# An encoder layer's FFN: loads of the next weight pair ahead of the stores, residual loaded into the sums, four early weight sums on VectorE

## The chip, the core and the metric

The kernel runs on one NeuronCore of a Trainium2 chip. The core has five engines that run at the same time, each with its own in-order list of instructions: TensorE (PE in the profile; PEld is its weight load), VectorE (DVE), ScalarE (ACT), GpSimd (POOL) and SyncE (SP), which here issues nearly all DMA transfers. The metric is the device time of one execution in microseconds (us); lower is better.

## The reference

Two requests of 1024 tokens (`x_prompt`, `x_sample`) go through one post-norm encoder layer with the same weights. The attention part takes about a third of the kernel's code and isn't touched here. The part that the change touches is the last one:

```
D_MODEL, D_FF, SEQ = 1024, 4096, 1024
x = layer_norm(ALPHA * x + merged @ w_out, ln1_g, ln1_b)
hid = square(relu(x @ w_ff1 + b_ff1))                          # FFN layer 1: 1024 -> 4096
x = layer_norm(ALPHA * x + hid @ w_ff2 + b_ff2, ln2_g, ln2_b)  # FFN layer 2: 4096 -> 1024
```

All of it is float32. The term `ALPHA * x + b_ff2` that is added to the second product is called the residual below.

## The kernel before

The two requests (batches, `b` = 0 and 1) are worked through one after the other by the same code. Every float32 product is made of three products of a high and a low part (`mm3`, lines 107 to 109: hi x hi, lo x hi, hi x lo). `split` (line 745) makes the parts: ScalarE copies the high part (line 746), VectorE subtracts it for the low part (line 103, the helper `sub`).

A matrix product is done by Strassen's scheme in Winograd's form: seven products of half-size blocks instead of eight, with sums of blocks before and after.

**FFN layer 1** runs over `NP` = 16 pairs `p` of 128-column blocks of `w_ff1`. A pair has two loads of 512 KB, `top` (tile `w1t`, two buffers) and `bot` (tile `w1b`, one buffer). `job_a` makes products 1 and 2 from `top`. `job_b` makes the sums of blocks (tile `ss`, line 905 on), their splits (`oh`, `ol`; for the block `a22` the tiles `o`), five more products and the sums behind them, and writes seven blocks (`c11`, `ht`) to HBM with `put` (line 878). `job_a` of the first four pairs (`EARLY`) is done ahead. The tile `w1b` is last read by the split of `a22`, so the next `w1b` load has to wait for that split on VectorE.

In the pairs 4 to 11, behind each job, one eighth of the residual is made (lines 949 to 962): `rg` (scale and shift, broadcast over the partitions, two loads of 256 KB) and `rr` (512 KB of the normalised rows, tensor `resd`) are loaded, GpSimd multiplies and adds in four operations, and the result is stored back into `resd`.

**FFN layer 2** runs over four chunks `c` of 1024 rows of `w_ff2`, in each over the seven products m = 1, 2, 6, 5, 3, 7, 4 with two halves `u`, and four token tiles `t`. `operands` loads the weights (tile `rw`) and the hidden blocks (tile `hr`), forms sums of weight blocks (called T sums; `ts` and rewritten `rw`), and splits. For the first chunk the sums of `u` = 0 are on VectorE and those of `u` = 1 on GpSimd (line 1009); later chunks have both on GpSimd. `product` adds each product to `acc` in SBUF with VectorE (line 1052). In the first chunk the first addition to each quarter of `acc` reads the residual instead of `acc`: it is loaded for that, in sixteen loads of 256 KB (tile `r`, three buffers, line 1051).

**What sets the order.** The kernel is written with a scheduler that simulates the program and writes each engine's list in the order that comes out; the order of the source gives the priorities. SyncE's list is then worked off strictly in order: a DMA whose wait isn't over holds up every DMA behind it.

Of the kernel before, what the change touches and what calls it, by code (L numbers as in the profile page):

```python
# [9 lines left out]
F32 = mybir.dt.float32  # L10
# [71 lines left out]
def encoder_kernel(ctx, tc, xs, w_in, b_gate, w_a, w_b, w_out, rpb, ln1_g, ln1_b, w1, b1, w2, b2,  # L82
# [184 lines left out]
    for b, x in enumerate(xs):  # L267
# [627 lines left out]
        zp.release()  # L895
        pup = pool("pu", 1, side="right")
        htp = pool("ht", 8, side="right")

        def job_b(p, top, px, c11):
            bot = bop.tile([P, KT, P], F32, name="w1b", tag="w1b")  # L900
            nc.sync.dma_start(bot, w1[:, (2 * p + 1) * P:(2 * p + 2) * P].rearrange("(k p) c -> p k c", p=P))
            ss = sp_.tile([P, 4, 4, P], F32, name="ss", tag="ss")
            s2, s1, s3, s4 = (ss[:, i] for i in range(4))
            a11, a12, a21, a22 = top[:, :4], top[:, 4:], bot[:, :4], bot[:, 4:]
            nc.vector.tensor_tensor(s1, a21, a22, op=ALU.add)
            sub(nc.vector, s2, s1, a11)
            sub(nc.vector, s3, a11, a21)
            sub(nc.vector, s4, a12, s2)
            o65 = w1_ops(ss[:, 0:2].rearrange("p i k c -> p (i k) c"), nc.vector)
            o73 = w1_ops(ss[:, 2:4].rearrange("p i k c -> p (i k) c"), nc.vector)  # L910
            o4 = [opq.tile([P, 4, P], F32R, name=f"o4{s}", tag=f"o4{s}") for s in range(2)]
            split(*o4, a22, nc.vector)
            relu2(c11, c11, 2 * p)
            put(p, 1, c11)
            u2, u3, p5 = (pup.tile([P, 512], F32, name=n, tag=n) for n in ("u2", "u3", "p5"))
            prod(px, [t[:, :4] for t in o65], xb[6], False)
            nc.scalar.copy(u2, px)
            py = psy.tile([P, 512], F32, name="py", tag="py")
# [17 lines left out]
            sub(nc.vector, h2, h1, c11)  # L936
            put(p, 6, h2)
            sub(nc.vector, h3, c11, c12)
            put(p, 7, h3)
            sub(nc.vector, h4, c21, h2)  # L940
            put(p, 3, h4)

        for p in range(EARLY):
            job_b(p, w1_top(p), *early[p])
        for p in range(EARLY, NP):
            top = w1_top(p)
            job_b(p, top, *job_a(p, top))

            i = p - EARLY
            if i < 8:  # L950
                ns = slice(512 * (i // 4), 512 * (i // 4 + 1))
                its = slice(2 * (i % 4), 2 * (i % 4) + 2)
                gt = xp.tile([P, 2, 512], F32, name="rg", tag="x")
                for j in range(2):
                    v = agd[j, ns]
                    nc.sync.dma_start(gt[:, j], bass.AP(tensor=v.tensor, offset=v.offset, ap=[[0, P], [1, 512]]))
                rt = xp.tile([P, 2, 512], F32, name="rr", tag="x")
                nc.sync.dma_start(rt, resd[b][its, :, ns].rearrange("t p c -> p t c"))
                for j in range(2):
                    nc.gpsimd.tensor_tensor(rt[:, j], rt[:, j], gt[:, 0], op=ALU.mult)  # L960
                    nc.gpsimd.tensor_tensor(rt[:, j], rt[:, j], gt[:, 1], op=ALU.add)
                nc.sync.dma_start(resd[b][its, :, ns].rearrange("t p c -> p t c"), rt)
        psz.release()
        psy.release()
        psx.release()
        for q in (htp, pup, opq, opp, awp, c11p, sp_, bop, xbp):
            q.release()


# [4 lines left out]
        ac0p = pool("acc0")  # L974
        acc = [pl.tile([P, 4, 2, 512], F32, name=f"acc{i}") for i, pl in enumerate((ac0p, accp))]

        padp = pool("pad")
        padp.tile([P, 512], F32, name="pad")
        w2b = pool("w2b", 2)
        w2a = pool("w2a", 2, side="right")  # L980
        hrp = pool("hr", 4, side="right")
        w2r = pool("w2r", 2, side="right")
        rsp = pool("res", 3, side="right")
        jkp = pool("junk", side="right")
        psx = pool("ps_x", 4, space=PSUM)
        psr = pool("ps_r", 2, space=PSUM)
# [8 lines left out]
        for c in range(nch):  # L995
# [7 lines left out]
            def operands(n, m, u):  # L1003
                w = rw[u]
                for j, d in {1: ((0, 0),), 2: ((1, 0),), 6: ((0, 1), (1, 1))}.get(m, ()):
                    w[j, d] = (w2r if d else w2b if j else w2a).tile([P, 2, 512], F32, name=f"rw{j}{d}", tag=f"rw{j}{d}")
                    nc.sync.dma_start(w[j, d], w2v[u, j, :, :, 512 * d:512 * (d + 1)])
                b11, b12, b21, b22 = (w.get(i) for i in ((0, 0), (0, 1), (1, 0), (1, 1)))
                eng = nc.gpsimd if c or u else nc.vector
                if m == 6:  # L1010
                    for i in (5, 6):
                        w[i] = w2r.tile([P, 2, 512], F32, name=f"ts{i}", tag=f"ts{i}")
                    sub(eng, w[5], b12, b11)
                    sub(eng, w[6], b22, w[5])
# [12 lines left out]
                split(o[:, 0], o[:, 1], hr, nc.vector)  # L1027
                split(o[:, 2], o[:, 3], src, nc.vector)

            def product(m, t):  # L1030

                if m == 1:
                    px[t] = psx.tile([P, 512], F32, name="px", tag="px")
                if m in (1, 6, 7, 4):
                    ps = px[t]
                else:
                    pl, tag = ((pst, "pt"), (psr, "pr"))[t % 2]
                    ps = pl.tile([P, 512], F32, name=tag, tag=tag)
                cs = slice(t * P, (t + 1) * P)
                for u in range(2):  # L1040
                    o = ops[m, u]
                    for q in range(2):
                        mm3(ps, o[:, 0, q, cs], o[:, 1, q, cs], o[:, 2, q], o[:, 3, q], m not in (6, 7, 4) and u + q == 0,
                            u + q == 2, skip=True)
                for s_ in {1: (0,), 2: (0,), 6: (1,), 5: (1, 3), 3: (1,), 7: (3,), 4: (2,)}[m]:
                    a = acc[s_ // 2][:, t, s_ % 2]
                    r = a
                    if c == 0 and (m, s_) in ((1, 0), (6, 1), (5, 3), (4, 2)):
                        r = rsp.tile([P, 512], F32, name="r", tag="r")
                        ns = slice(512 * (s_ % 2), 512 * (s_ % 2 + 1))  # L1050
                        nc.sync.dma_start(r, resd[b][t + 4 * (s_ // 2), :, ns])
                    nc.vector.tensor_tensor(a, r, ps, op=ALU.add)
                if last and (m == 3 or m == 4 and b + 1 == len(xs)):
                    finish(m == 4, t)

            for n, m in enumerate((1, 2, 6, 5, 3, 7, 4)):
                for u in range(2):
                    operands(n, m, u)
                if not last or n < 5:
                    for t in range(4):  # L1060
                        product(m, t)
# [4 lines left out]
        psr.release()  # L1066
        psx.release()
        pst.release()
        for q in (jkp, rsp, w2r, hrp, w2a, w2b, padp, ac0p):
            q.release()  # L1070
        if b + 1 == len(xs):
            lnp.release()
# [41 lines left out]
```

## Time and profile before

| | us |
|---|---|
| median of 3 runs | 3175.51 |
| range of the runs | 3169.77 to 3178.15 |
| the profiled execution, its own time | 3184.45 |
| span of the profiled execution | 3182.6 |
| TensorE busy in it | 2951.2 (93% of the span) |
| VectorE / ScalarE / GpSimd busy | 1881.0 / 1449.7 / 979.1 |

Times in the trace count from the start of the span. FFN layer 1 of the first batch stands at about 950 to 1283 us and layer 2 at 1283 to 1500 us and on; of the second batch at about 2510 to 2840 us and 2840 to 3165 us. A row of the timeline gives the start, the duration, the engine, the line, the operation, the tiles, and in brackets how long the engine was idle before it and what ended that. SPq is SyncE's queue of DMA issues: its duration is that of the issue, not of the transfer. The view of stretches gives for each stretch the busy time of each engine with the number of its instructions, TensorE's granted clock as a share of full speed, the mean busy share of the DMA engines, and GB/s.

### The profile page before, as it was taken

To read this page: it belongs to the slowest core of one execution; us is meant where nothing else is said; L and a number is where in the kernel's file an instruction comes from. 1 tells how busy PE (TensorE), PEld (TensorE's weight loads), DVE (VectorE), ACT (ScalarE), POOL (GpSimd) and SP (SyncE) were. 2 spreads that over 40 slices of the span, in tenths; PEclk is the share of its full clock that TensorE was granted. 3 is DMA by queue.
4 is the path that set the end of the run, shared out by engine and by line. 5 is a ranking of instruction groups with operands and counts; after the bars stand their busy time and mean duration, and the time that the engine had idled before them with its cause. 6 is when DMAs were issued, how large, how long until landed. Compare 5 with 4: busy or idle time off the path is not lost. (4 is left out here: it accounts for less than half of the span.)

```text
span 3182.6 us, 39432 instructions
## 1 busy us (share of the span) xinstructions
PE 2951.2 (93%) x13964; PEld 2441.7 (77%) x13964; DVE 1881.0 (59%) x3439; ACT 1449.7 (46%) x2640; POOL 979.1 (31%) x716
## 2 busy tenths in 40 slices
PE   7879898999997899899989998989999979998997
PEld 7757786888786788688878786878877767886886
DVE  1036566673465666687861565567444756558887
ACT  3136564554363455333441564646542735553333
POOL 3464563223203200133341655432130131004322
PEclk9989898999998999899999999989999989999998
DMA  8742224345546644654354123244454575466442
GB/s 182 255 130 81 74 71 119 119 131 189 174 143 189 201 159 159 237 177 155 96 195 141 56 79 90 66 135 121 158 157 151 169 226 191 146 210 208 148 139 86
DMA packets 404414, 470.22 MB, mean 148 GB/s; under 512 B 44841, under 2 KB 282225, under 8 KB 403961
## 3 DMA queue, kind: packets, MB, share of 16 engines
q1 hardware_dynamic: 377720, 429.43, 43.1%
q10 hardware_dynamic: 26496, 38.28, 3.6%
q8 instruction: 110, 1.80, 0.2%
q14 instruction: 88, 0.71, 0.1%
HBM read 326.77 MB, written 141.79 MB: 147 GB/s over the span
## 5 line engine op out<-in xcount | busy, mean ns | idle before, releaser
L107 PE MATMUL pmm<-bh,whi 128*128 128x512 f32 x1152 | 465.4, 404 | 29.5 <-ACT r L451 23.6
L108 PE MATMUL pmm<-bh,wlo 128*128 128x512 f32 x1152 | 463.2, 402 | 0.0
L109 PE MATMUL pmm<-bl,whi 128*128 128x512 f32 x1152 | 462.7, 402 | 0.0
L103 POOL TENSOR_TENSOR wlo<-wraw,whi 128x512 fp32r<-128x512 f32 (+1 forms) x176 | 231.8, 1331 | 533.0 <-ACT whi L195 493.1
L107 PEld LDWEIGHTS pmm<-bh,whi 128*128 128x128 f32 x1152 | 221.1, 192 | 72.8 <-ACT r L451 24.9
L109 PEld LDWEIGHTS pmm<-bl,whi 128*128 128x128 f32 x1152 | 220.9, 192 | 42.7
L108 PEld LDWEIGHTS pmm<-bh,wlo 128*128 128x128 f32 x1152 | 221.0, 192 | 40.3
L103 POOL TENSOR_TENSOR ts<-rw,rw 128x1024 f32<-128x1024 f32 x14 | 41.4, 2957 | 655.7 <-DMA rw<-in_w_ff_dram 497.4
L746 ACT CAST bh<-hr 128x1024 fp32r<-128x1024 f32 x56 | 58.7, 1048 | 366.0 <-PE px L109 216.9
L391 ACT ACTIVATE smk<-smk,nm 128x256 f32<-128x256 f32 (+4 forms) x320 | 162.0, 508 | 129.1 <-DVE nm L390 126.1
L103 DVE TENSOR_TENSOR ptl<-pt,pth 128x512 fp32r<-128x512 f32 (+3 forms) x224 | 125.3, 569 | 67.4 <-ACT pth L667 36.7
L107 PE MATMUL psv<-wv,bh 128*128 128x384 f32 (+1 forms) x384 | 139.7, 365 | 19.8 <-DVE vt L103 18.2
L103 DVE TENSOR_TENSOR vt<-psv,vt 128x384 fp32r<-128x384 f32 (+1 forms) x48 | 28.8, 602 | 214.4 <-ACT vt L342 214.4
L108 PE MATMUL psv<-wv,bl 128*128 128x384 f32 (+1 forms) x384 | 139.9, 364 | 0.3 <-DVE bl L103 0.3
L109 PE MATMUL psv<-wv,bh 128*128 128x384 f32 (+1 forms) x384 | 138.5, 363 | 1.6 <-POOL wv L103 1.5
L107 PE MATMUL px<-bh,oh 128*128 128x512 f32 x256 | 106.4, 416 | 32.4 <-ACT oh L746 25.3
L103 POOL TENSOR_TENSOR qs<-r,qs 64x512 fp32r<-64x512 f32 x80 | 116.8, 1460 | 63.2 <-ACT qs L414 58.9
L108 PE MATMUL px<-bh,ol 128*128 128x512 f32 x256 | 105.6, 413 | 20.1 <-DVE ol L103 20.1
L746 ACT CAST oh<-ss 128x1024 fp32r<-128x1024 f32 x64 | 66.9, 1053 | 123.9 <-DVE ss L103 93.7
L103 DVE TENSOR_TENSOR bh<-hr,bh 128x1024 fp32r<-128x1024 f32 x56 | 84.0, 1500 | 57.5 <-ACT bh L746 57.4
L107 PE MATMUL pso<-woh,bh 128*128 128x512 f32 x256 | 103.9, 406 | 11.8 <-DVE sg L720 11.8
L960 POOL TENSOR_TENSOR rr<-rr,rg 128x512 f32<-128x512 f32 x32 | 48.7, 1542 | 212.1 <-DMA rr<-resd 199.0
(283 smaller groups left out, 8480.7 us busy)
## 6 DMA issues: line engine op xcount, KB each, us to landing
hr<-hidd SPq DMA_DIRECT2D x112, 512.0 KB
hidd<-ht SPq DMA_DIRECT2D x192, 256.0 KB
wraw<-in_w_in_dram SPq DMA_DIRECT2D x144, 256.0 KB
rw<-in_w_ff_dram SPq DMA_DIRECT2D x64, 512.0 KB
w1t<-in_w_ff_dram SPq DMA_DIRECT2D x40, 512.0 KB
gd<-gt ACTq DMA_DIRECT2D x32, 512.0 KB
sg<-gd SPq DMA_DIRECT2D x32, 512.0 KB
w1b<-in_w_ff_dram SPq DMA_DIRECT2D x32, 512.0 KB
```

Of the source, the lines that this page charges most:

```text
L103: eng.tensor_tensor(out, a, b, op=ALU.subtract)
L107: nc.tensor.matmul(out, ah, bh, start=start, stop=False, skip_group_check=skip)
L108: nc.tensor.matmul(out, al, bh, start=False, stop=False, skip_group_check=skip)
L109: nc.tensor.matmul(out, ah, bl, start=False, stop=stop, skip_group_check=skip)
L391: nc.scalar.activation(pr[:, e0:e1], pr[:, e0:e1], AF.Exp, bias=nm, scale=1.0, accum_out=den)
L746: nc.scalar.copy(oh, src)
L960: nc.gpsimd.tensor_tensor(rt[:, j], rt[:, j], gt[:, 0], op=ALU.mult)
```

## The change

In FFN layer 1 the load of `bot` moves out of `job_b` into `w1_bot`. Both loads of pair p + 1 now stand in `job_b(p)` behind the split of `a22` and ahead of the stores. The residual's work is cut in two: `residual_load` stands in `job_b` at the same place, `residual` (GpSimd's four operations and the store) behind the job. `rg` is loaded once for four pieces instead of for each, and `rr` has a pool of its own with one buffer.

In FFN layer 2 `start_sum` loads the residual straight into the quarters of `acc`, in four loads of 1 MB, one behind the operands of each of the first four products; the additions then all read `acc`, and the tile `r` is gone. The T sums of the first chunk are now all on VectorE.

```diff
+        def w1_bot(p):
             bot = bop.tile([P, KT, P], F32, name="w1b", tag="w1b")
             nc.sync.dma_start(bot, w1[...])
+            return bot
+
+        def job_b(p, top, px, c11):
+            bot = bots.pop(p)
...
             split(*o4, a22, nc.vector)
+
+            if p + 1 < NP:
+                tops[p + 1] = w1_top(p + 1)
+                bots[p + 1] = w1_bot(p + 1)
+            residual_load(p - EARLY)
             relu2(c11, c11, 2 * p)
             put(p, 1, c11)
...
+        def residual_load(i):
+            if not 0 <= i < 8:
+                return
+            ns = slice(512 * (i // 4), 512 * (i // 4 + 1))
+            if i % 4 == 0:
+                res["g"] = gt = xp.tile([P, 2, 512], F32, name="rg", tag="x")
                 for j in range(2):
                     v = agd[j, ns]
                     nc.sync.dma_start(gt[:, j], bass.AP(...))
+            res["t"] = rt = rsp.tile([P, 2, 512], F32, name="rr", tag="rr")
+            nc.sync.dma_start(rt, resd[b][...])
...
+        for p in range(NP):
+            top = tops.pop(p)
+            job_b(p, top, *(early[p] if p < EARLY else job_a(p, top)))
+            residual(p - EARLY)
...
+        def start_sum(h, j):
+            nc.sync.dma_start(acc[h][:, :, j], resd[b][...])
...
-                eng = nc.gpsimd if c or u else nc.vector
+                eng = nc.gpsimd if c else nc.vector
...
-                    if c == 0 and (m, s_) in ((1, 0), (6, 1), (5, 3), (4, 2)):
-                        r = rsp.tile([P, 512], F32, name="r", tag="r")
-                        nc.sync.dma_start(r, resd[b][...])
-                    nc.vector.tensor_tensor(a, r, ps, op=ALU.add)
+                    nc.vector.tensor_tensor(a, a, ps, op=ALU.add)
...
                 for u in range(2):
                     operands(n, m, u)
+                if c == 0 and n < 4:
+                    start_sum(*((0, 0), (0, 1), (1, 1), (1, 0))[n])
```

What the scheduler makes of it is seen best on SyncE's list. The first place is layer 1 of the first batch, from the second residual load up to the `w1b` load of pair 2. Before (hidd are the stores of `put`, resd<-rr the residual's store):

```order
L958 DMA rr<-resd_83 128x2x512
L878 DMA hidd_81<-ht 128x512
L962 DMA resd_83<-rr 128x2x512
L878 DMA hidd_81<-ht 128x512
L956 DMA rg<-agd 128x512
L878 DMA hidd_81<-ht 128x512 x4
L901 DMA w1b<-in_w_ff_dram 128x8x128
```

The same place after the change:

```order
L966 DMA rr<-resd_83 128x2x512
L878 DMA hidd_81<-ht 128x512 x5
L902 DMA w1b<-in_w_ff_dram 128x8x128
L878 DMA hidd_81<-ht 128x512
L975 DMA resd_83<-rr 128x2x512
L966 DMA rr<-resd_83 128x2x512
```

The residual's store, which waits for GpSimd, has moved from ahead of the `w1b` load to behind it, and the `rg` loads there are gone. Numbering the eight residual pieces 0 to 7: in the first batch the last piece stored ahead of the `w1b` loads of the pairs 2 to 7 was 1, 1, 3, 5, 6, 7 and is now 0, 1, 3, 4, 5, 7. In the second batch it is 1, 1, 3, 5, 6, 7 before and after.

The second place is SyncE's list at the start of layer 2 of the first batch, up to the first weight load of product 6 (rw). Before:

```order
L1024 DMA hr<-hidd_81 128x2x512
L193 DMA wraw<-in_w_in_dram 128x4x128
L878 DMA hidd_81<-ht 128x512
L1024 DMA hr<-hidd_81 128x2x512 x2
L1051 DMA r<-resd_83 128x512 x3
L1007 DMA rw_11584<-in_w_ff_dram 128x2x512
```

The same place after, where acc is the sum in SBUF, g and bb the constants of the second layer norm, and wraw a load for the next batch:

```order
L998 DMA acc_11385<-resd_83 128x4x512
L878 DMA hidd_81<-ht 128x512 x2
L998 DMA acc_11385<-resd_83 128x4x512
L878 DMA hidd_81<-ht 128x512
L1047 DMA hr<-hidd_81 128x2x512
L263 DMA g_12945<-in_ln_g_dram 128x1024
L1047 DMA hr<-hidd_81 128x2x512
L878 DMA hidd_81<-ht 128x512
L263 DMA bb_12947<-in_ln_b_dram 128x1024
L193 DMA wraw<-in_w_in_dram 128x4x128 x3
L1047 DMA hr<-hidd_81 128x2x512 x3
L1030 DMA rw_11561<-in_w_ff_dram 128x2x512
```

All four loads into acc (two more stand just above these rows) are now ahead of the weights of product 6, where three loads of a quarter of their size stood, and one more load of hr is ahead of them too.

The third place is VectorE's list from the first T sum of the first batch on. Before:

```order
L103 TENSOR_TENSOR ts_11588<-rw_11584,rw_11428 128x1024
L103 TENSOR_TENSOR bl_11683<-hr,bl_11683 128x1024
L103 TENSOR_TENSOR ts_11589<-rw_11586,ts_11588 128x1024
L103 TENSOR_TENSOR rw_11584<-rw_11586,rw_11584 128x1024
L103 TENSOR_TENSOR bh_11676<-ts_11588,bh_11676 128x1024
L1052 TENSOR_TENSOR acc_11398<-r,px 128x512
L103 TENSOR_TENSOR rw_11510<-rw_11510,ts_11589 128x1024
L103 TENSOR_TENSOR bl_11683<-ts_11603,bl_11683 128x1024
L103 TENSOR_TENSOR bh_11594<-ts_11589,bh_11594 128x1024
L1052 TENSOR_TENSOR acc_11398<-acc_11398,pr 128x512
L103 TENSOR_TENSOR bl_11609<-ts_11604,bl_11609 128x1024
```

After, with the four sums of the second half (ts_11580, ts_11581, rw_11576, rw_11495) that were on GpSimd:

```order
L103 TENSOR_TENSOR ts_11565<-rw_11561,rw_11411 128x1024
L103 TENSOR_TENSOR ts_11566<-rw_11563,ts_11565 128x1024
L103 TENSOR_TENSOR rw_11561<-rw_11563,rw_11561 128x1024
L103 TENSOR_TENSOR bh_11646<-ts_11565,bh_11646 128x1024
L103 TENSOR_TENSOR rw_11486<-rw_11486,ts_11566 128x1024
L103 TENSOR_TENSOR ts_11580<-rw_11576,rw_11420 128x1024
L103 TENSOR_TENSOR bh_11571<-ts_11566,bh_11571 128x1024
L103 TENSOR_TENSOR ts_11581<-rw_11578,ts_11580 128x1024
L103 TENSOR_TENSOR rw_11576<-rw_11578,rw_11576 128x1024
L103 TENSOR_TENSOR bl_11653<-ts_11580,bl_11653 128x1024
L103 TENSOR_TENSOR rw_11495<-rw_11495,ts_11581 128x1024
L103 TENSOR_TENSOR bl_11586<-ts_11581,bl_11586 128x1024
```

VectorE now has twelve operations from the first T sum to the last low part of products 5 and 6, where it had nine and two additions to acc.

## Rows read from the trace of the kernel before

**Rows 1.** The page's first line.

```profile
span 3182.6 us, 39432 instructions
```

**Rows 2.** Stretches of both batches: us, then PE, PEld, DVE, ACT, POOL; clock; DMA.

```profile
980.00:1020.00 40.00, 24.20 (x91) 18.77 (x90) 23.78 (x23) 11.26 (x17) 13.76 (x10) 0.74 0.64 204
1060.00:1100.00 40.00, 31.00 (x112) 23.73 (x111) 28.38 (x30) 19.30 (x29) 14.59 (x8) 0.83 0.59 185
1110.00:1260.00 150.00, 150.00 (x657) 123.09 (x656) 88.85 (x121) 82.16 (x127) 0.00 (x0) 1.00 0.47 151
1270.00:1300.00 30.00, 29.27 (x128) 23.52 (x127) 14.94 (x16) 14.34 (x19) 0.00 (x0) 1.00 0.93 329
1300.00:1330.00 30.00, 16.27 (x47) 11.72 (x46) 24.82 (x18) 6.18 (x6) 12.54 (x4) 0.66 0.61 214
2540.00:2580.00 40.00, 23.10 (x90) 18.02 (x90) 23.48 (x24) 12.30 (x19) 13.79 (x9) 0.79 0.67 212
2620.00:2660.00 40.00, 30.99 (x118) 23.40 (x117) 28.60 (x30) 19.30 (x29) 15.23 (x8) 0.87 0.61 194
...
2860.00:2890.00 30.00, 20.95 (x73) 15.60 (x72) 25.45 (x20) 6.28 (x6) 12.84 (x4) 0.83 0.55 198
```

**Rows 3.** Waits of SyncE's queue, 940 to 1110: us in total, times, longest.

```profile
SPq L962 <- POOL rr L961: 38.1, 7, 7.1
```

**Rows 4.** SyncE's queue in the timeline, layer 1, first batch.

```profile
969.12 0.37 SPq L962 DMA_DIRECT2D resd<-rr  x1
...
973.05 0.37 SPq L958 DMA_DIRECT2D rr<-resd  x1
...
984.28 0.37 SPq L962 DMA_DIRECT2D resd<-rr  x1
...
989.33 0.44 SPq L901 DMA_DIRECT2D w1b<-in_w_ff_dram  x1
...
1052.18 0.37 SPq L962 DMA_DIRECT2D resd<-rr  x1
...
1055.37 0.64 SPq L901 DMA_DIRECT2D w1b<-in_w_ff_dram  x1
...
1251.77 0.40 SPq L901 DMA_DIRECT2D w1b<-in_w_ff_dram  x1
```

**Rows 5.** VectorE in the timeline, layer 1, first batch.

```profile
983.02 1.78 DVE L103 TENSOR_TENSOR o<-w1b,o 128x512 fp32r<-128x512 f32 x1
...
995.81 0.69 DVE L905 TENSOR_TENSOR ss<-w1b 128x512 f32<-128x512 f32 x1 [8.07 <-DMA w1b<-in_w_ff_dram]
...
1046.24 1.80 DVE L103 TENSOR_TENSOR o<-w1b,o 128x512 fp32r<-128x512 f32 x1
...
1256.53 0.69 DVE L905 TENSOR_TENSOR ss<-w1b 128x512 f32<-128x512 f32 x1 [3.41 <-DMA w1b<-in_w_ff_dram]
```

**Rows 6.** TensorE in the timeline, both layers, first batch.

```profile
998.84 0.80 PE L107 MATMUL px<-bh,oh 128*128 128x512 f32 x1 [9.67 <-ACT oh L746]
...
1006.18 0.79 PE L108 MATMUL px<-bh,ol 128*128 128x512 f32 x1 [6.12 <-DVE ol L103]
...
1312.35 0.80 PE L107 MATMUL pt<-bh 128*128 128x512 f32 x1 [7.48 <-ACT bh L746]
```

**Rows 7.** GpSimd in the timeline: residual in layer 1, T sum in layer 2.

```profile
998.01 3.10 POOL L960 TENSOR_TENSOR rr<-rr,rg 128x512 f32<-128x512 f32 x2 [13.76 <-DMA rr<-resd]
...
1310.70 2.73 POOL L103 TENSOR_TENSOR ts<-rw,rw 128x1024 f32<-128x1024 f32 x1 [216.55 <-DMA rw<-in_w_ff_dram]
```

**Rows 8.** SyncE's queue, layer 1, second batch.

```profile
2547.57 0.37 SPq L962 DMA_DIRECT2D resd<-rr  x1
...
2551.72 0.84 SPq L901 DMA_DIRECT2D w1b<-in_w_ff_dram  x1
```

**Rows 9.** VectorE in the timeline, start of layer 2, first batch.

```profile
1310.00 1.22 DVE L103 TENSOR_TENSOR ts<-rw,rw 128x1024 f32<-128x1024 f32 x1
1311.13 3.38 DVE L103 TENSOR_TENSOR bl<-hr,bl 128x1024 fp32r<-128x1024 f32 x1
...
1328.92 1.21 DVE L103 TENSOR_TENSOR bl<-ts,bl 128x1024 fp32r<-128x1024 f32 x1
```

More of the change, by code (lines that the diff above doesn't have):

```diff
@@ L897, in encoder_kernel @@
         htp = pool("ht", 8, side="right")
-        def job_b(p, top, px, c11):
+        rsp = pool("res", 1, side="right")
+        def w1_bot(p):
             bot = bop.tile([P, KT, P], F32, name="w1b", tag="w1b")
             nc.sync.dma_start(bot, w1[:, (2 * p + 1) * P:(2 * p + 2) * P].rearrange("(k p) c -> p k c", p=P))
+            return bot
+        def job_b(p, top, px, c11):
+            bot = bots.pop(p)
             ss = sp_.tile([P, 4, 4, P], F32, name="ss", tag="ss")
@@ L941, in job_b @@
             put(p, 3, h4)
[L943 to L953, printed above, removed]
+        res = {}
+        def residual_load(i):
[4 more added lines that the diff above has]
+                res["g"] = gt = xp.tile([P, 2, 512], F32, name="rg", tag="x")
                 for j in range(2):
@@ L956, in encoder_kernel, with residual @@
                     nc.sync.dma_start(gt[:, j], bass.AP(tensor=v.tensor, offset=v.offset, ap=[[0, P], [1, 512]]))
[L957 to L962, printed above, removed]
+            res["t"] = rt = rsp.tile([P, 2, 512], F32, name="rr", tag="rr")
+            nc.sync.dma_start(rt, resd[b][2 * (i % 4):2 * (i % 4) + 2, :, ns].rearrange("t p c -> p t c"))
+        def residual(i):
+            if not 0 <= i < 8:
+                return
+            gt, rt = res["g"], res["t"]
+            for j in range(2):
+                nc.gpsimd.tensor_tensor(rt[:, j], rt[:, j], gt[:, 0], op=ALU.mult)
+                nc.gpsimd.tensor_tensor(rt[:, j], rt[:, j], gt[:, 1], op=ALU.add)
+            nc.sync.dma_start(resd[b][2 * (i % 4):2 * (i % 4) + 2, :, 512 * (i // 4):512 * (i // 4 + 1)].rearrange("t p c -> p t c"), rt)
+        tops, bots = {0: w1_top(0)}, {0: w1_bot(0)}
+        for p in range(NP):
+            top = tops.pop(p)
+            job_b(p, top, *(early[p] if p < EARLY else job_a(p, top)))
+            residual(p - EARLY)
         psz.release()
@@ L965, in encoder_kernel @@
         psx.release()
-        for q in (htp, pup, opq, opp, awp, c11p, sp_, bop, xbp):
+        for q in (rsp, htp, pup, opq, opp, awp, c11p, sp_, bop, xbp):
             q.release()
@@ L975, in encoder_kernel @@
         acc = [pl.tile([P, 4, 2, 512], F32, name=f"acc{i}") for i, pl in enumerate((ac0p, accp))]
+        def start_sum(h, j):
+            nc.sync.dma_start(acc[h][:, :, j], resd[b][4 * h:4 * h + 4, :, 512 * j:512 * (j + 1)].rearrange("t p c -> p t c"))
         padp = pool("pad")
@@ L982, in encoder_kernel @@
         w2r = pool("w2r", 2, side="right")
-        rsp = pool("res", 3, side="right")
         jkp = pool("junk", side="right")
@@ L1046, in product @@
                     a = acc[s_ // 2][:, t, s_ % 2]
-                    r = a
-                    if c == 0 and (m, s_) in ((1, 0), (6, 1), (5, 3), (4, 2)):
-                        r = rsp.tile([P, 512], F32, name="r", tag="r")
-                        ns = slice(512 * (s_ % 2), 512 * (s_ % 2 + 1))
-                        nc.sync.dma_start(r, resd[b][t + 4 * (s_ // 2), :, ns])
-                    nc.vector.tensor_tensor(a, r, ps, op=ALU.add)
+                    nc.vector.tensor_tensor(a, a, ps, op=ALU.add)
                 if last and (m == 3 or m == 4 and b + 1 == len(xs)):
@@ L1068, in encoder_kernel @@
         pst.release()
-        for q in (jkp, rsp, w2r, hrp, w2a, w2b, padp, ac0p):
+        for q in (jkp, w2r, hrp, w2a, w2b, padp, ac0p):
             q.release()
```

## The prediction

> **What bounds the kernel now.** I read the share of TensorE first, then stretches of time, then the queues at the stretches that stand out. TensorE is busy for 93% of a span of 3182.6 us [rows 1]; in its full flow it issues 657 matmuls in 150 us, 4.38 in a microsecond, and idles not at all [rows 2]. So time can come only from the stretches where it falls short of that. The part that the change touches has six. From 980 to 1020 us 91 matmuls ran where 175 fit, so 84 are missing, 84/4.38 = 19.2 us. In the same way 1060 to 1100 lacks 63 (14.4 us), 2540 to 2580 lacks 85 (19.4 us), 2620 to 2660 lacks 57 (13.0 us): 66 us in layer 1 of both batches. At the start of layer 2, 1300 to 1330 lacks 84 of 131 (19.2 us) and 2860 to 2890 lacks 58 (13.3 us): 32 us. The counts include what the clock costs: it was granted at 0.66 to 0.87 of full speed in these stretches and at 1.00 in the full flow [rows 2], that is, TensorE ran part of them at 1.2 GHz after its waits. Whether a stretch shrinks is a question of what ends its wait last.
>
> In layer 1 that is the load of `w1b`. VectorE's first sum of pair 2 starts at 995.81 after waiting for it, and TensorE's two waits, 9.67 and 6.12 us, end at 998.84 and 1006.18 with the split parts made from these sums [rows 5, 6]. The load could have been issued when the split that last reads the buffer ended, 983.02 + 1.78 = 984.8; it was issued at 989.33, because the residual's store ahead of it waited for GpSimd until 984.28 and the stores of the hidden blocks stood behind that [rows 4, 5]. SyncE's queue stood for 38.1 us in seven such waits for GpSimd [rows 3]. At the start of layer 2 it is the weights of product 6 and the T sums made of them: TensorE runs out, waits 7.48 us, and starts at 1312.35 behind a sum that VectorE began at 1310.00 [rows 6, 9].
>
> **Layer 1, first batch.** In the new queue the store of piece 1 stands behind the load for pair 2. Issue: 984.8 instead of 989.33, 4.5 us earlier. Transfer: it took 995.81 - 989.33 = 6.5 us with four stores just in front; a load in the full flow took 1256.53 - 1251.77 = 4.8 us [rows 4, 5]. It lands near 989.6. From there to TensorE's full flow took 1006.18 - 995.81 = 10.4 us, because GpSimd's residual work began at 998.01 [rows 7], beside VectorE's sums and splits, and stretched them; the next piece now starts behind the load, at about 995, when these are nearly done. I take 5 us, half. Full flow at 994.6 instead of 1006.2: 11 us.
>
> For pair 5 the split ended at 1046.24 + 1.80 = 1048.0 and the load was issued at 1055.37, behind the store of piece 5 at 1052.18 [rows 4, 5]: 7.3 us late. Now only piece 4 is ahead. But `rr` has one buffer, so a residual load waits until the store before it is done, 973.05 - 969.12 = 3.9 us [rows 4], and holds the queue while it does; and GpSimd's piece 5 will run beside the sums of pair 5. I leave 6 of the 14.4 us in place: 8 us.
>
> **Layer 1, second batch.** Here the scheduler left the residual's stores where they were against the `w1b` loads. The load for pair 2 was issued 2551.72 - 2547.57 = 4.2 us behind the store [rows 8]; fewer stores and no `rg` load stand between now. I take 2 us from that, 2 us from a shorter transfer and 2 us from GpSimd starting later: 6 of 19.4 us. For pairs 5 and 6 the store of pieces 5 and 6 still waits for GpSimd ahead of the load: 3 of 13.0 us. Together layer 1 gives 11 + 8 + 6 + 3 = 28 us. Its bounds: nothing, if another wait takes the place of each, and 55 us, the 66 us less about 11 us of sums, splits and clock that no load order removes. I take 28, as it is built from rows of the same places.
>
> The moved loads themselves cost no bandwidth: the DMA engines are 59 to 67% busy in these stretches [rows 2], and twelve `rg` loads of 256 KB a batch go away. In the full flow from 1110 us nothing waits and I cost the new order at nothing; TensorE's own work covers it.
>
> **Layer 2, the loads.** The DMA engines are 93% busy at 329 GB/s from 1270 to 1300 [rows 2], so full is 329/0.93 = 354 GB/s, and what stands ahead of a load delays it by its bytes. Ahead of the weights of product 6 stand now 4 MB of residual instead of three loads of 256 KB, and in the first batch one more load of 512 KB: 3.4 MB in one batch, 3.9 MB in the other, 9.6 and 11 us at 354 GB/s, less some 2 us of capacity that was idle. I charge 9 us a batch.
>
> **Layer 2, the sums.** VectorE needed from 1310.00 to 1328.92 + 1.21 = 1330.1, 20.1 us, for nine operations of 1024 columns and two additions. An operation next to GpSimd's sums, which start at 1310.70, takes 3.38 us where it takes 1.22 alone [rows 7, 9]. Now there are twelve, one every 1.13 us (1311.13 - 1310.00): 13.6 us, 6.5 us less. The sum of 1310.00 stood behind additions that wait for `r`, and that wait goes: 0.5 us. So layer 2 costs 9 - 7 = 2 us a batch, 4 us in all, with bounds of -14 (the weights are not later) and +22 (they are 11 us later and the shorter chain helps nobody).
>
> The Trainium skill (Perfetto Trace Analysis, Optimizing Scalar/DVE Operations) says that GpSimd and VectorE share a read port of SBUF, so that moving operations from one to the other might not help. By that the chain stays at 20.1 us and layer 2 would cost 13 us more than my sum, near rival 3; the trace agrees about the sharing (3.38 against 1.22 us), but a T sum on GpSimd took 2.73 us [rows 7] against 1.22 on VectorE by itself, so the move should gain here, and I keep 13.6 us.
>
> **The sum.** -28 + 4 = -24 us. Against the profiled execution's own 3184.45 us that is 3160; it stands 0.3% above the median of the runs, and against the median, 3175.51, it is 3152 us.
>
> **Rivals.** (1) *The queue comes free altogether.* If GpSimd's pieces drift behind all sums of layer 1, also in the second batch, layer 1 gives about 50 us and layer 2 nothing: 3126 us. For it: the seven waits of 38.1 us; against it: the second batch's order. (2) *One wait takes the place of the other.* Seven residual loads a batch now wait 3.9 us each for the store before them, 27 us of a standing queue against the 38.1 us for GpSimd. If these fall ahead of the `w1b` loads, layer 1 gives 5 us and layer 2 takes 4: 3175 us, no change. For it: the single buffer. (3) *Slower: the residual ahead of the weights.* If product 6's weights come 11 us later in each batch and TensorE, already out of work, waits for all of that, while the shorter chain of sums is hidden behind its slow restart, layer 2 costs 22 us; with 10 us from layer 1 that is 3188 us. It decides from the point at which layer 1 gives less than layer 2 takes. For it: the DMA engines are full just there. Against it: the four stretches of layer 1 hold twice as much as those of layer 2.
>
> The Trainium skill (Perfetto Trace Analysis, DMA Optimizations) notes that splitting a DMA into smaller pieces may let the work start sooner; the change merges sixteen pieces into four and puts them ahead of the weights, which by this is the wrong way round, and speaks for rival 3. No row before shows 1 MB loads there.
>
> **How the numbers follow.** My forecast, a gain of 10 to 45 us, has 0.50; rival 1 0.16; rival 2 0.19; rival 3 0.15. A measurement of this kernel can tell some 0.3%, 9.5 us, from no change. Faster by more: the forecast, rival 1 and a little of rival 2, 0.68; within: 0.17; slower by more: 0.15. The range reaches from rival 1 (3126, a little below it for its own spread) to between rivals 2 and 3: 3122 to 3180.
>
> **What would show it.** Right in layer 1: in the first batch the `w1b` load of pair 2 is issued within 1 us of the split's end, and the four stretches lack about 38 us of matmuls instead of 66. Wrong: the queue's waits for the residual's store or load stay near 38 us a batch. Right in layer 2: GpSimd has no T sum before the second chunk, VectorE's operations there take 1.2 us, and the first T sum starts some 6 to 9 us later after TensorE ran out than now. Wrong: that delay is over 12 us, or TensorE's wait for product 6's weights grows past 16 us. A new wait in the full flow of layer 1, where there was none, would upset all of it.

## The result and the profile after

The changed kernel takes 3144.0 us in the median of four runs (3140.6 to 3147.5) against 3176.8 of the kernel before: a ratio of 0.9894 with a 95% interval of 0.9879 to 0.9909, 33 us less. The forecast was 3152, 24 us less. A later set of runs gave 3146.8 against 3176.3, ratio 0.9913 (0.9899 to 0.9928). The profiled execution took 3147.5 us, its first lines on the page are these (busy time, share of the span, instructions):

```profile
span 3145.6 us, 39383 instructions
PE 2943.3 (94%) x13964; PEld 2438.1 (78%) x13964; DVE 1864.7 (59%) x3447; ACT 1449.0 (46%) x2640; POOL 953.1 (30%) x708
```

TensorE's work is the same; 37 us of span went with its idle time and its slow clock. Where they went is seen in stretches that start at the same work in both kernels. Four stretches of before: 160 us of layer 1 (from 16 us ahead of pair 1's first sum) in each batch, then 110 us of each batch's layer 2, from some 35 us ahead of the moment at which TensorE runs out of work. The columns are those of [rows 2].

```profile
940.00:1100.00 160.00, 132.43 (x526) 104.71 (x525) 96.75 (x111) 75.66 (x125) 49.17 (x32) 0.87 0.60 187
2504.00:2664.00 160.00, 131.31 (x544) 103.89 (x543) 97.53 (x111) 76.68 (x127) 51.16 (x32) 0.91 0.62 196
1270.00:1380.00 110.00, 94.97 (x388) 75.25 (x386) 79.64 (x69) 37.70 (x43) 32.54 (x10) 0.91 0.69 234
2830.00:2940.00 110.00, 98.58 (x411) 78.88 (x410) 84.05 (x76) 40.14 (x45) 31.79 (x10) 0.95 0.68 232
```

The same four of after:

```profile
934.00:1094.00 160.00, 148.57 (x610) 117.66 (x609) 110.50 (x124) 85.03 (x141) 53.06 (x32) 0.95 0.57 189
2470.00:2630.00 160.00, 138.82 (x571) 110.84 (x570) 99.00 (x119) 78.84 (x131) 48.66 (x32) 0.91 0.56 186
1247.00:1357.00 110.00, 96.91 (x413) 78.49 (x413) 80.10 (x83) 38.97 (x44) 21.28 (x7) 0.94 0.74 256
2793.00:2903.00 110.00, 97.02 (x413) 78.72 (x412) 81.78 (x85) 39.69 (x46) 20.32 (x7) 0.94 0.71 245
```

More matmuls in equal time is time won, at 4.38 a microsecond: 84 in layer 1 of the first batch (19 us), 27 in the second (6 us), 25 in the first layer 2 (6 us), 2 in the second (0.5 us). Layer 1 of the second trace of after gives 71 and 34 matmuls (16 and 8 us):

```profile
938.00:1098.00 160.00, 146.69 (x597) 116.33 (x596) 109.26 (x125) 84.70 (x139) 51.01 (x32) 0.94 0.57 190
2474.00:2634.00 160.00, 137.74 (x578) 109.90 (x578) 97.89 (x119) 80.40 (x135) 46.43 (x32) 0.94 0.57 186
```

So layer 1 gave 24 to 25 us here, and of the 66 us that it lacked some 41 are left, where the prediction had 38.

A second reading follows the whole span: the **lead**, the start of one and the same operation in before less its start in another kernel. The markers are the first sum from `w1b` of pair 1 and of pair 15 in each batch (956.04, 1256.53, 2519.95, 2817.00 us in before), a copy of layer 2's last chunk (1499.82) and VectorE's last operation (3175.90). The growth of the lead between two markers is what a stage gained, in us:

| kernel | median, us | ratio to before | ahead of it | layer 1, b 0 | layer 2, b 0 | between | layer 1, b 1 | layer 2, b 1 |
|---|---|---|---|---|---|---|---|---|
| after | 3144.0 | 0.9894 | 5.6 | 17.3 | 8.5 | 2.3 | 2.2 | 1.1 |
| after, second trace | 3146.8 | 0.9913 | 2.4 | 15.6 | 6.5 | 5.0 | 6.5 | 2.1 |
| e1 layer 1 alone | 3146.8 | 0.9906 | 7.0 | 14.8 | 1.5 | -2.1 | 12.7 | -2.4 |
| e2 layer 2 alone | 3165.3 | 0.9974 | 1.3 | 0.1 | 5.0 | 2.5 | -0.3 | 3.0 |
| e3 T sums as before | 3148.7 | 0.9921 | -0.1 | 16.5 | 2.3 | 1.4 | 8.4 | -0.8 |
| e4 residual as before | 3136.8 | 0.9882 | 3.4 | 20.6 | 6.6 | 2.3 | 14.7 | 4.7 |
| e5 `rr` from two buffers | 3154.0 | 0.9935 | 8.4 | 8.0 | 6.7 | -0.1 | 6.5 | 4.5 |
| e6 stores on GpSimd | 3135.3 | 0.9877 | 4.3 | 23.0 | 2.1 | 1.4 | 20.5 | -0.3 |
| e7 no residual | 3108.0 | 0.9789 | 8.2 | 35.1 | 7.8 | 2.6 | 23.4 | 2.2 |
| e8 no GpSimd work | 3136.3 | 0.9870 | 6.7 | 20.5 | 4.6 | 4.6 | 15.2 | 1.4 |
| e9 e4 and e6 | 3124.6 | 0.9839 | 7.4 | 21.5 | 6.6 | 1.9 | 21.2 | -0.8 |
| e10 residual late | 3143.7 | 0.9889 | 4.4 | 10.7 | 10.0 | 0.6 | 8.2 | 5.9 |
| e12 loads on GpSimd too | 3133.8 | 0.9877 | 3.1 | 26.0 | 3.4 | 2.4 | 17.3 | 1.0 |

The columns "ahead of it" and "between" hold work that no edit touches: up to 8 us there are spread between executions, and before's profiled execution stood 8 us above its median. So the stages of after hold 29 us (31 in its second trace) of the 37, and a single stage is known to 2 to 4 us. Of the second trace 17 to 20, 3 to 9 and 5 to 8 us were expected, before it was run, in layer 1 of the first and the second batch and in layer 2 of the first; the first of these was missed (15.6).

After's lead in layer 1 of the second batch includes a loss that isn't a wait. In the full flow behind the stretch TensorE ran 516 matmuls in 120 us in after, without a wait and at a granted clock of 1.00, and 526 in its second trace, as in before (657 in 150 us [rows 2]):

```profile
2655.00:2775.00 120.00, 120.00 (x516) 97.21 (x515) 69.33 (x94) 63.72 (x98) 0.00 (x0) 1.00 0.46 147
2655.00:2775.00 120.00, 120.00 (x526) 98.45 (x525) 71.50 (x96) 65.70 (x102) 0.00 (x0) 1.00 0.47 149
```

Counting matmuls in order, after's lead fell by 2.7 us between the matmuls that start at 2680 and at 2820 us in before, and that of the second trace stayed the same. Why TensorE was slower there stays open. So the 2.2 us in the table stand for some 6, as the stretches have it.

**Layer 1.** SyncE's queue in the first batch, and in the second:

```profile
977.86 0.38 SPq L902 DMA_DIRECT2D w1b<-in_w_ff_dram  x1
...
980.72 0.37 SPq L975 DMA_DIRECT2D resd<-rr  x1
...
2502.81 0.36 SPq L975 DMA_DIRECT2D resd<-rr  x1
2505.55 0.36 SPq L966 DMA_DIRECT2D rr<-resd  x1
...
2515.14 0.37 SPq L975 DMA_DIRECT2D resd<-rr  x1
...
2517.64 0.63 SPq L902 DMA_DIRECT2D w1b<-in_w_ff_dram  x1
```

The splits that free `w1b` there, on VectorE:

```profile
976.05 1.78 DVE L103 TENSOR_TENSOR o<-w1b,o 128x512 fp32r<-128x512 f32 x1
...
2509.07 0.68 DVE L103 TENSOR_TENSOR o<-w1b,o 128x512 fp32r<-128x512 f32 x1
```

In the first batch the split ends at 976.05 + 1.78 = 977.83 and the load is issued 0.03 us later, the residual's store behind it; in before it was 4.5 us late [rows 4, 5]. In the second batch the split ends at 2509.75, the store stands ahead as before and is let go at 2515.14, and the load is 7.9 us late. In before it was 8.3 us late: the split there ended at 2543.42, the load was issued at 2551.72 [rows 8]. TensorE's waits show the same (idle time and what ended it in brackets, first pair 2 of each batch, then product 6):

```profile
985.11 0.50 PE L107 MATMUL px<-bh,oh 128*128 128x512 f32 x1 [1.51 <-ACT oh L746]
2525.84 0.79 PE L107 MATMUL px<-bh,oh 128*128 128x512 f32 x1 [7.91 <-ACT oh L746]
...
1292.37 0.79 PE L107 MATMUL pt<-bh 128*128 128x512 f32 x1 [11.34 <-ACT bh L746]
...
2838.53 0.80 PE L107 MATMUL pt<-bh 128*128 128x512 f32 x1 [11.66 <-ACT bh L746]
```

The 9.67 us of [rows 6] are 1.51; the second batch still waits 7.91. The queue itself waits hardly less than in [rows 3] (940 to 1110 us: total, times, longest):

```profile
SPq L975 <- POOL rr L974: 35.4, 8, 7.6
...
SPq L966 <- DMA resd<-rr: 10.1, 5, 4.1
```

Only what stands behind these waits has changed.

**Layer 2.** TensorE ran out at 1292.37 - 11.34 = 1281.03. The first T sum and the last low part of the chain on VectorE:

```profile
1290.01 1.23 DVE L103 TENSOR_TENSOR ts<-rw,rw 128x1024 f32<-128x1024 f32 x1 [6.27 <-DMA rw<-in_w_ff_dram]
...
1302.80 1.22 DVE L103 TENSOR_TENSOR bl<-ts,bl 128x1024 fp32r<-128x1024 f32 x1
```

The sum starts 9.0 us after TensorE ran out (5.1 in before: 1310.00 in [rows 9], less 1304.87, which is [rows 6]'s start less its wait). The twelve operations take 14.0 us where nine and two additions took 20.1.

### The profile page after: what moved, and what is told of

Same layout as the page of the kernel before. It is cut to its first block, busy times and chain, and to the rows that moved or that the text cites. A ratio compares the mean times of both kernels' runs of the same rounds, so it can differ in the third digit from the quotient of the medians.

```text
span 3145.6 us, 39383 instructions
## 1 busy us (share of the span) xinstructions
PE 2943.3 (94%) x13964; PEld 2438.1 (78%) x13964; DVE 1864.7 (59%) x3447; ACT 1449.0 (46%) x2640; POOL 953.1 (30%) x708
## 5 line engine op out<-in xcount | busy, mean ns | idle before, releaser
L103 POOL TENSOR_TENSOR ts<-rw,rw 128x1024 f32<-128x1024 f32 x12 | 33.8, 2815 | 668.1 <-DMA rw<-in_w_ff_dram 295.9
L107 PE MATMUL px<-bh,oh 128*128 128x512 f32 x256 | 105.7, 413 | 19.5 <-ACT oh L746 10.1
L107 PE MATMUL pso<-woh,bh 128*128 128x512 f32 x256 | 104.4, 408 | 12.7 <-DVE sg L720 12.7
L342 ACT CAST vt<-psv 128x384 fp32r<-128x384 f32 (+1 forms) x48 | 24.6, 516 | 177.1 <-PE psv L109 78.8
```

Of the source, the lines that this page charges most:

```text
L103: eng.tensor_tensor(out, a, b, op=ALU.subtract)
L107: nc.tensor.matmul(out, ah, bh, start=start, stop=False, skip_group_check=skip)
L342: nc.scalar.copy(vt[:, :2 * npair, 0], pv)
```

## The experiments

Each kernel was run next to the kernel before, whose median in these sets was 3172.7 (e1 to e4), 3176.3 (second run of after, e5 to e7), 3177.8 (e8 to e10) and 3173.4 us (e12).

**e1 and e2: one layer alone.** The two halves of the diff, each with the other layer of the kernel before.

> Layer 1 of the change with layer 2 of the kernel before. Theory (the order of loads and stores in layer 1 gives what the lead of after over before grows by there, 18.5 us in the first batch and 3.5 in the second; layer 2 gives the rest): 22 us under before, 3155 us, and at the start of layer 2 TensorE waits some 7 us as before. Rival (the growth of the lead in layer 2 is spread between runs, all of the 33 us come from layer 1): 3144 us.

> Layer 1 of the kernel before with layer 2 of the change. Theory: the lead grew by 7.4 us over layer 2 of the first batch and by 0 over that of the second, so 3170 us, 7 under before. Rival (my prediction, 2 us a batch the other way): 3181 us. Either way layer 1 keeps its waits of 9.7 and 6.1 us for the w1b load of pair 2.

e1 took 3146.8 us, ratio 0.9906 (0.9890 to 0.9921); e2 3165.3, ratio 0.9974 (0.9964 to 0.9984). e2's time agrees with the theory, 7 us, though they came from both batches. e1 gave 26 instead of 22, so its time is nearer to the rival's 3144 than to the theory's 3155, but not for the rival's reason, since e2 shows that layer 2 gives something by itself. As expected, layer 2 gave nothing in e1, but layer 1 of the second batch gave 12.7 instead of 2 to 6. There the scheduler had put the stores of the pieces 1, 5 and 6 behind the loads of the pairs 2, 5 and 6, as in the first batch, and the load of pair 2 was issued with no delay. The source of layer 1 is the same as in after. So what sets the batches of after apart is above all this order in SyncE's queue, which an edit in layer 2 can turn over.

**e3 and e4: the two edits of layer 2 apart.**

In e3:

```diff
-                eng = nc.gpsimd if c else nc.vector
+                eng = nc.gpsimd if c or u else nc.vector
```

In e4:

```diff
-                if c == 0 and n < 4:
-                    start_sum(...)
+                        r = rsp.tile([P, 512], F32, name="r", tag="r")
+                        nc.sync.dma_start(r, resd[b][...])
```

> The change, but the T sums of the first chunk's second half go back to GpSimd. Theory (the shorter chain of sums gave back 11 us after TensorE's wait in the first batch and 5 in the second): 16 us over after, 3160 us, and VectorE's operations of 1024 columns beside GpSimd's sums take some 3.4 us again. Rival (the sums are hidden either way, layer 2 gains from the loads into acc): 3144 us.

> The change, but the residual is loaded in sixteen loads of 256 KB for the first additions, as before. Theory (4 MB ahead of the weights of product 6 make them some 4 to 5 us later in each batch): 9 us under after, 3135 us, and TensorE's wait at the start of layer 2 is about 7 us instead of 11 to 12. Rival (the additions that wait for small loads cost VectorE as much): 3144 us or more.

e3 took 3148.7 us, ratio 0.9921 (0.9907 to 0.9936): 2 to 5 us over after, which the intervals can't tell from nothing, and not 16. e4 took 3136.8, ratio 0.9882 (0.9867 to 0.9897), close to what was expected. But only part of it is layer 2: in e4 the scheduler again turned the order of the second batch's layer 1, which gained 14.7 us. The stretches of 110 us in layer 2 tell the edits apart, both batches, of e1 (neither edit), e3 (loads into `acc` alone) and e4 (sums alone):

```profile
1247.00:1357.00 110.00, 93.00 (x382) 73.68 (x381) 80.15 (x71) 36.25 (x43) 31.36 (x10) 0.91 0.69 233
2794.00:2904.00 110.00, 97.51 (x399) 77.61 (x398) 83.69 (x75) 41.78 (x48) 31.97 (x10) 0.91 0.64 224
```

```profile
1254.00:1364.00 110.00, 93.61 (x394) 74.90 (x393) 81.90 (x74) 38.86 (x45) 31.96 (x10) 0.94 0.70 242
2800.00:2910.00 110.00, 94.27 (x403) 76.22 (x402) 83.79 (x77) 39.81 (x47) 32.04 (x10) 0.95 0.67 237
```

```profile
1246.00:1356.00 110.00, 96.94 (x409) 76.49 (x409) 76.51 (x80) 39.83 (x46) 17.09 (x6) 0.97 0.73 253
2777.00:2887.00 110.00, 102.54 (x435) 82.68 (x434) 82.64 (x85) 45.69 (x54) 19.07 (x6) 0.97 0.69 240
```

Means over both batches: with neither edit (before and e1) 395 matmuls, loads alone 398.5, sums alone 422, both (after) 413. So the sums are worth 27 matmuls without the loads (6.2 us a batch) and 14.5 with them (3.3 us); the loads are worth 3.5 without the sums (0.8 us, within the spread) and cost 9 with them (2 us). Stretches of the same code in the same batch differ by up to 12 matmuls, so each of these is known to some 2 us. The sums' gain is clear of that; the loads' cost is not. By the table, layer 2 of both batches gained 11.3 us in e4 against 9.6 and 8.6 in after, and 5.8 in e9 (below) against 1.8 in e6, which differ in the same way: 1 to 2 us a batch.

**e5: the single buffer of `rr`.** `rr` is taken from the pool `xp`, which has two buffers, as before the change.

```diff
-            res["t"] = rt = rsp.tile([P, 2, 512], F32, name="rr", tag="rr")
+            res["t"] = rt = xp.tile([P, 2, 512], F32, name="rr", tag="x")
```

> The change, but rr is taken from the pool of two buffers that it had before; the scheduler then puts the store of piece 1 ahead of the w1b load of pair 2 in both batches, and the store of piece 3 ahead of that of pair 4. Theory (a w1b load behind a residual store is what costs): layer 1 of the first batch loses 8 to 10 of its 18.5 us, 3153 us. Rival (the waits of residual loads for the stores before them, on one buffer, hold the queue): 3140 us or less.

3154.0 us, ratio 0.9935 (0.9920 to 0.9950), as the theory had it: layer 1 of the first batch gained 8.0 us instead of some 16, and the load of pair 2 came 4.5 us late again. The scheduler had put the residual's stores back ahead of the loads of the pairs 2, 5 and 6, as in before, so this order is worth 8 to 9 us in the first batch. The other 8 us came without it; what they are due to (the `rg` loads that are gone, the loads issued ahead of the stores of `put`) wasn't tested. On balance the change's one buffer is no cost here, since with it the scheduler orders the loads of the first batch well.

**e6: the stores leave SyncE's queue.**

```diff
-            nc.sync.dma_start(resd[b][...], rt)
+            nc.gpsimd.dma_start(resd[b][...], rt)
```

> The change, but GpSimd issues the residual's stores itself, so no store in SyncE's queue waits for GpSimd. Theory: the w1b load of pair 2 of the second batch is issued within 1 us of the split's end, and layer 1 of that batch gains 10 us as in e1 and e4: 3134 us. Rival (the residual loads, which wait for the single buffer, take the place of the stores): 3144 us or more.

3135.3 us, ratio 0.9877 (0.9859 to 0.9895), as expected: the load of pair 2 of the second batch was 1.0 us late, and layer 1 gained 23.0 and 20.5 us. The rival shows too, without deciding: the queue's wait for the residual's stores is now on the loads (940 to 1110 us),

```profile
SPq L966 <- DMA resd<-rr: 36.9, 7, 9.9
```

and the `w1b` load of pair 6 was 6.5 us late behind one of them.

**e7 and e8: what the residual costs in layer 1.** e7 leaves the eight pieces out, e8 only GpSimd's four operations on each.

> The change with the residual's eight pieces left out of layer 1 (no loads, no work on GpSimd, no stores; layer 2 starts from the rows as they stand in memory). It shows how much the residual still costs there. Theory (loads wait behind it and VectorE is slowed by GpSimd beside it): layer 1 gains another 15 us in the first batch and 25 in the second, 3104 us. Rival (the pairs without the first two products are bound by the one w1b buffer and the sums anyway): 3135 us.

> The change with GpSimd's four operations on each residual piece left out: the pieces are loaded and stored as they are, so loads and stores remain, and layer 2 starts from unscaled rows. The scheduler moves the stores a little earlier, since they wait for less. Theory (what the residual still costs is GpSimd's work: the waits for it and VectorE slowed beside it): close to the run without any residual, 3110 us. Rival (the traffic and the queue of loads and stores cost it): 3130 us or more.

e7 took 3108.0 us, ratio 0.9789 (0.9774 to 0.9804), close to the theory: the residual still costs after 36 to 39 us (against either median of it). e8 took 3136.3, ratio 0.9870 (0.9856 to 0.9883), and there the theory fell: without any work on GpSimd, the loads and stores still cost 26 to 28 us against e7 (by the ratios and by the medians). How much of that is the queue's order and how much the traffic itself isn't told apart. The stores now wait for the loads ahead of them (first row, 940 to 1110 us), and pair 4's `w1b` load, issued at 1019.36, was 6.8 us late behind such a store:

```profile
SPq L972 <- DMA rr<-resd: 22.8, 8, 4.8
...
1012.58 0.36 SPq L966 DMA_DIRECT2D rr<-resd  x1
...
1016.63 0.37 SPq L972 DMA_DIRECT2D resd<-rr  x1
...
1019.36 1.00 SPq L902 DMA_DIRECT2D w1b<-in_w_ff_dram  x1
```

**e9: e4 and e6 together.**

> Both edits that helped, together: the residual's stores are issued by GpSimd (e6), and the residual is added from sixteen small loads (e4). Theory (they act at different stages): 9 us from the stores in the second batch and the first, 8 us from the loads in layer 2: 3128 us, and at the start of layer 2 TensorE waits 3 to 7 us instead of 11 to 15. Rival (the earlier end of layer 1 runs into the same loads): 3135 us, as e6.

3124.6 us (3123.2 to 3133.3), ratio 0.9839 (0.9825 to 0.9852): the fastest kernel of this study that computes everything, 53 us under the median of before in its set. TensorE's waits at the start of layer 2 were 5.7 and 2.9 us.

**e10: the residual in the full flow.** e9, with

```diff
-            residual_load(p - EARLY)
+            residual_load(p - 7, ss)
...
+            nc.gpsimd.tensor_copy(rt[:, 0, :1], ss[:, 0, 0, :1])
             nc.sync.dma_start(rt, resd[b][...])
...
-            residual(p - EARLY)
+            residual(p - 7)
```

> e9, and the residual's pieces move from the pairs 1 to 7 to the pairs 7 to 14, where TensorE ran without idling: one element of GpSimd's tile is first written from the sums of that pair, so that its load waits for them. Theory (only the place is wrong: in the full flow GpSimd's work and its loads are covered): 20 us under e9, 3108 us. Rival (in the full flow it costs as much, as the w1b loads there have no time to spare either): 3128 us or more.

3143.7 us, ratio 0.9889 (0.9876 to 0.9903): the theory fell. The pairs up to 7 run nearly as in e7, but the full flow, 657 matmuls in 150 us in before [rows 2], is gone:

```profile
936.00:1096.00 160.00, 155.83 (x667) 125.98 (x667) 100.94 (x135) 91.34 (x149) 10.84 (x9) 0.98 0.49 155
1110.00:1260.00 150.00, 138.93 (x578) 110.84 (x577) 100.44 (x105) 74.71 (x115) 49.31 (x36) 0.97 0.57 187
```

79 matmuls, 18 us. The reason is seen on VectorE and GpSimd in one pair of it:

```profile
1182.38 3.01 POOL L974 TENSOR_TENSOR rr<-rr,rg 128x512 f32<-128x512 f32 x2 [4.36 <-DMA rr<-resd]
1185.35 3.40 POOL L975 TENSOR_TENSOR rr<-rr,rg 128x512 f32<-128x512 f32 x2
```

```profile
1185.86 1.76 DVE L103 TENSOR_TENSOR ht<-c,ht 128x512 f32<-128x512 f32 x1
1187.54 0.67 DVE L890 TENSOR_TENSOR c<-c,pz 128x512 f32<-128x512 f32 x1
1188.14 1.16 DVE L103 TENSOR_TENSOR o<-w1b,o 128x512 fp32r<-128x512 f32 x1
```

While GpSimd runs, an operation of VectorE that reads two tiles in SBUF takes 1.76 us instead of 0.69, and the split of `a22` stands behind several of these. So the next `w1b` load starts late, in pairs that had nothing to spare.

**e12: the loads leave the queue as well.** e9, with

```diff
-            nc.sync.dma_start(rt, resd[b][...])
+            nc.gpsimd.dma_start(rt, resd[b][...])
```

> e9, and GpSimd issues the residual's loads too, so nothing of the residual waits in SyncE's queue. It tells what the queue still costs (the w1b load of pair 6 was issued 5.7 us after the split's end in e9) from what GpSimd's work costs beside VectorE. Theory: the load of pair 6 is issued within 1 us, which gives 3 to 5 us in each batch, and the rest of the 17 us a batch up to the run without residual is GpSimd's: 3117 us. Rival (the queue is all of it): 3100 us. Rival (GpSimd's pieces come at the worst places again): 3125 us or more.

3133.8 us, ratio 0.9877 (0.9857 to 0.9897): slower than e9, so the theory fell. Pair 6's load was 1.0 us late in the first batch, and layer 1 there gained 26.0 us, 4.5 more than e9. But the wait came back elsewhere. A load of `hr` takes the buffer of `rg`; in SyncE's queue it waited 13.4 us for GpSimd's last reading (940 to 1110 us), and pair 8's `w1b` load behind it was 4.3 us late:

```profile
SPq L1043 <- POOL rr L974: 14.2, 2, 13.4
...
1085.50 0.37 SPq L1043 DMA_DIRECT2D hr<-hidd  x1
...
1093.34 0.69 SPq L902 DMA_DIRECT2D w1b<-in_w_ff_dram  x1
```

That doesn't make up 9 us; the second batch lost 3.9 us against e9 in layer 1, the first one 3.2 in layer 2, and 4.3 lie ahead of all edits. Why e12 as a whole is slower stays open.

## Why the prediction was right

The time lay within the range, 8 us under the forecast, and the sign was right. Step by step:

1. **Layer 1, first batch: 11 + 8 = 19 us forecast; 17.3 and 15.6 measured.** Right, by the mechanism named: the load of pair 2 is issued 0.03 us after the split's end, and TensorE's first wait fell from 9.67 to 1.51 us. e5 puts the stores back ahead of the loads and takes half of the gain away. The two terms were off in opposite ways. Counting matmuls in order, between those that start at 940 and 1040 us in before, the place of pair 2, the lead grew by 14.3 us (12.4 in the second trace), and from there to 1120 us by 4.8 (3.7). The load of pair 5 is 0.6 us late instead of 7.3, but those of the pairs 4 and 7 are 2.7 and 4.1 us late (1.3 for pair 7 in the second trace), where they were 1.9 and 1.0.
2. **Layer 1, second batch: 6 + 3 = 9 us forecast; 2.2 and 6.5 measured, 6 and 8 by the stretches, which end ahead of after's slow full flow.** The direction was right, the first term too large and the second too small: counted as above, 2500 to 2600 us gave 0.3 us (1.4 in the second trace) and 2600 to 2680 gave 5.6 (6.4), where the load of pair 6 is issued 0.7 us after the split instead of 4.3. Of the first term's three parts the load stood closer behind the store by 1.7 us (2.5 instead of 4.2) and the transfer was 1.1 us shorter (2 us each were forecast); from GpSimd nothing came, as TensorE's second wait there is 6.3 us instead of 6.1. But the store itself was let go later, 5.4 us after the split instead of 4.2: GpSimd's piece 1 had to wait for its load, and this, on the single buffer, for the store of piece 0 (2502.81, then 2505.55 in the queue rows above). That is rival 2's mechanism, and it decided this one place. e1 and e4, where the load of pair 2 stands ahead of the store, show 12.7 and 14.7 us.
3. **Layer 2, the loads: 9 us a batch forecast as a cost; 1 to 2 measured, no more than the spread, and none where the sums stay on GpSimd (e3 against e1).** This is the step that failed most. The prediction charged all bytes ahead of product 6's weights at 354 GB/s. By the rows, the first T sum came 3.9 us later after TensorE ran out in the first batch and 5.2 in the second, and a part of that was given back at once, since the sums behind it no longer waited for `r` or for GpSimd.
4. **Layer 2, the sums: 7 us a batch forecast; 3.3 measured with the loads into `acc`, 6.2 without.** The chain is 6.1 us shorter, as forecast (6.5). What the prediction left out is how TensorE restarts: in the first batch of before two more waits, 3.65 and 2.60 us, followed within 13 us of the first, at a granted clock of 0.50 and 0.61:

```profile
1318.93 0.80 PE L107 MATMUL px<-bh 128*128 128x512 f32 x1 [3.65 <-ACT bh L746]
...
1324.46 0.80 PE L109 MATMUL pt<-bh 128*128 128x512 f32 x1 [2.60 <-DVE bh L103]
```

   In after there is one wait, and 10 us later the clock is 1.00. The rows of 10 us, before from 1312 and 1322, then after from 1292 and 1302:

```profile
1312.00:1322.00 10.00, 5.86 (x12) 3.65 (x12) 10.00 (x4) 3.34 (x4) 9.92 (x4) 0.50 0.56 194
1322.00:1332.00 10.00, 7.54 (x22) 5.99 (x23) 8.14 (x7) 0.00 (x0) 1.32 (x1) 0.61 0.08 26
```

```profile
1292.00:1302.00 10.00, 9.63 (x33) 7.76 (x34) 10.00 (x10) 3.47 (x4) 0.00 (x0) 0.75 0.48 164
1302.00:1312.00 10.00, 10.00 (x46) 8.28 (x45) 6.87 (x7) 4.00 (x4) 0.52 (x1) 1.00 0.34 110
```

   There one longer wait was cheaper than three shorter ones: by the rows, TensorE ran at 1.2 GHz (0.63 us a matmul instead of 0.39) through all three, until 1329.74, and in after came back to 2.4 GHz 4.4 us after the one. The second batch of before had it milder, since the two later waits were short and TensorE was back at 2.4 GHz between them:

```profile
2874.07 0.80 PE L107 MATMUL px<-bh 128*128 128x512 f32 x1 [0.37 <-ACT bh L746]
...
2879.61 0.80 PE L109 MATMUL pt<-bh 128*128 128x512 f32 x1 [1.97 <-DVE bh L103]
```

   There the change gained 1.1 and 2.1 us, against 8.5 and 6.5 in the first batch. e1's second batch, with the code of before, had waits of 3.28, 4.79 and 2.60 us at 1.2 GHz throughout, and lost 2.4 us against before. One long wait alone isn't what gains: e3 has it too (11.3 and 11.2 us), but with two waits of 1.2 to 2.1 us behind it, and gained 2.3 and -0.8. So it takes the shorter chain of sums; that the clock makes up the difference between the batches is read from these rows and wasn't tested by itself.
5. **The sum.** 28 - 4 = 24 us forecast, 29 to 31 in the traces' stages: layer 1 gave 6 to 9 us less than forecast (3 to 4 by the stretches) and layer 2 some 13 more. The forecast's time was near because two misses stood against each other; to that extent it was luck.
6. **The rivals.** Rival 1 (the queue free, 3126): its price for layer 1, 50 us, was about right, as e9 (43) and e7 (59) show, but it takes other edits to get it. Rival 2 (a new wait in place of the old, 3175): its condition came true, the queue waits 35.4 + 10.1 us, yet not its time. "The queue's waits stay near 38 us" was a badly chosen sign against layer 1: they may stay if nothing urgent stands behind them. Rival 3 (the residual ahead of the weights, 3188): TensorE's wait grew as it said, from 7.5 to 11.3 and from 6.5 to 11.7 us, and e4 confirms that the loads hold it. But its price, 22 us in two batches, was 2 to 4, as only a part of the longer wait became lost time (step 3).
7. **The page on the shared port** (the Trainium skill, Perfetto Trace Analysis, Optimizing Scalar/DVE Operations): by it the move of the sums might not help. Here it helped by 3.3 to 6.2 us a batch. That splitting a DMA into smaller chunks may let some start sooner (the Trainium skill, Perfetto Trace Analysis, DMA Optimizations) agrees with e4's waits: with sixteen loads of 256 KB instead of four of 1 MB TensorE waited 6.2 and 2.9 us instead of 11.3 and 11.7. In time that gave 1 to 2 us a batch where VectorE had the sums, no more than the spread.

## What to carry to other kernels

In an in-order queue of DMAs, ask not how long it stands still but what stands behind the standing instruction: moving the loads of three pairs ahead of one store each was worth 6 to 9 us a batch (after against e5 in the first, e1 against after's second trace in the second), while the queue waited as long as before. A scheduler may turn that order over after an edit elsewhere, so read the queue's list in each loop and batch; taking the waiting stores out of that queue (e6) gained more here than placing them well. A gap in which TensorE waits several times in a row can cost more than the sum of its waits, as the clock may stay down between them; count matmuls in a stretch, not idle time.

## What the runs showed of the hardware

- In e10's rows GpSimd slows VectorE's operation on two tiles in SBUF (`ht<-c,ht`, 1.76 us) but not the one between them that reads one operand from PSUM (`c<-c,pz`, 0.67 us). The Trainium skill (SBUF — State Buffer, Who interferes with whom) says just this: an instruction of VectorE with two inputs in SBUF contends with one of GpSimd that reads SBUF, one with at most one such input doesn't. That makes it possible to choose what to run beside GpSimd.
- Work that is hidden in a stretch without any idling is not free: the eight residual pieces took 18 us of the full flow of the first batch in e10, though GpSimd had been idle there and the DMA engines were at 0.47.
- Two traces of one kernel agreed within 2 us in three of the four stages, and differed by 4.3 us in layer 1 of the second batch, with the same order of instructions. Of these, 2.7 us lie in a full flow without any wait, where one trace ran 516 matmuls in 120 us and the other 526, both at a granted clock of 1.00: the row of the clock doesn't tell all of TensorE's pace.
